# Second mixer: low parts of weights by VectorE, splits ahead of time, and a new spread of the recurrences' tasks

## The chip, the cores and the metric

One core of a Trainium2 chip. The metric is the time of the whole program on the device, in microseconds (us). TensorE multiplies matrices, VectorE and ScalarE do elementwise work on SBUF and PSUM, GpSimd elementwise work on SBUF; SyncE issues the transfers (DMA). Each engine runs its own instructions in the order in which they stand and waits at an instruction until the semaphores that it names are reached.

## The reference, cut to what matters

Two layers of a decoder trunk on 512 tokens of width 1024, float32. Each is a mixer and a mixture of experts (32 experts, top 2 of one group of 8), each with a normalisation ahead and a residual. The change stands in the second layer's mixer:

```python
def mixer_rglru(h, w_in, conv_w, conv_b, w_a, b_a, w_x, b_x, lam, w_out):
    gate, xr = jnp.split(h @ w_in, [D_RNN], axis=-1)       # (512, 1024) each
    gate = jax.nn.gelu(gate)
    xr = causal_conv(xr, conv_w) + conv_b                  # width 4, over positions
    xh = xr.reshape(bsz, t_len, LRU_HEADS, LRU_HEAD_DIM)   # 8 heads of 128
    r = jax.nn.sigmoid(einsum('bthi,hij->bthj', xh, w_a) + b_a)
    i = jax.nn.sigmoid(einsum('bthi,hij->bthj', xh, w_x) + b_x)
    log_a = (LRU_C * r) * jax.nn.log_sigmoid(lam)
    a = jnp.exp(log_a)
    b = jnp.sqrt(-jnp.expm1(2.0 * log_a)) * (i * xr)
    hseq = scan over positions of  s = a * s + b
    return (gate * hseq) @ w_out
```

## The kernel before, in words

`mixer0`, the experts of layer 0, `mixer1`, the experts of layer 1, and the final normalisation follow each other. Everything in a mixer stands with channels on the 128 partitions and the 512 tokens along the free dimension.

The product `h @ w_in` of `mixer1` is made in four parts of 512 columns, called products here: product 2 (columns of heads 0 to 3), product 3 (heads 4 to 7), then product 0 and product 1 (the gate's columns of the same heads). Each is one call of `unit`. It runs over eight row blocks of 128 rows (`j`), and a row block is 12 matmuls of 128x512: four column tiles (`m`) by three terms. The weight `w` is split for that: a high part `wh`, a cast by ScalarE (line 391), and a low part `wl = w - wh`, a subtraction by another engine (line 392); `h` is split the same way into `hh` and `hl`. The terms are high by high, high by low, low by high. In product 2 the low parts are VectorE's; in products 3, 0 and 1 they are GpSimd's (`lo=G`). `unit` splits one row block ahead: the split of block `j + 1` is written before the matmuls of block `j`. High and low parts have two buffers each, in turn. A product's four results stand in four PSUM banks, 0 to 3 for products 2 and 0, 4 to 7 for 3 and 1.

After each row block `unit` takes tasks from a list (`pump`); `queue` fills this list with one slot per row block. So the tasks of slot `j` stand, on each engine, behind the split of block `j + 1` and the matmuls of block `j`, and ahead of the split of block `j + 2`. The tasks of a head `h` are:

- `conv` (c): an ACTIVATE (line 580), then three steps on VectorE that read the product's bank (line 583).
- `gates` (g): two matmuls (line 591), a tanh by ScalarE on each (line 595). The gates of heads 4 and 5 write banks 4 and 5, where the results of product 3 for heads 4 and 5 stand until their `conv` has read them.
- `decay` (d): a tanh and an exponential by ScalarE (lines 601, 602), three steps on VectorE (lines 604 to 606).
- `newton` (w): three steps on VectorE (lines 610 to 612), the last one `q = -2q - 1`.
- `roots`: for four heads at once a table load, four square roots by ScalarE (line 616), and a load of the next table.
- `scan` (s): two steps on VectorE (lines 620, 621).
- `gated` (e): gelu of the gate by ScalarE, a product on VectorE, and the split of the result `y` into a high part (cast, line 464) and a low part (line 465) for the next product. For heads 0 to 3 GpSimd makes that low part.

Heads 0 to 3 have their conv, gates, decay and newton in product 3; heads 4 to 7 have theirs in product 0, with the scans of heads 0 to 3, and end in product 1.

Then `project` multiplies `y` by `w_out` in 16 pieces of 12 matmuls (line 691): the first two pieces need heads 0 to 3 of `y`, the next two heads 4 to 7. After them the experts' first steps are mixed in. The experts' weights come through a ring of ten buffers of 1 MB and some buffers of the mixer: the first lands in buffer `D1`, which holds heads 4 to 7 of the recurrence until the mixer's end.

Of the kernel before, what the change touches and what calls it, by code (L numbers as in the profile page):

```python
# [8 lines left out]
F32 = mybir.dt.float32  # L9
F32R = mybir.dt.float32r  # L10
# [29 lines left out]
def hybrid_trunk(ctx: ExitStack, tc: tile.TileContext, x, norm_mix_g, norm_ffn_g, norm_final_g,  # L40
# [289 lines left out]
    class Normed:  # L330
# [52 lines left out]

    par = [0]

    def split(w, lo):
        par[0] += 1
        shape = [P, *w.shape[1:]]
        wh = big.tile(shape, F32R, tag=f"w{par[0] % 2}", name="wh")
        wl = big.tile(shape, F32R, tag=f"w{par[0] % 2 + 2}", name="wl")  # L390
        A.copy(wh, w)  # L391
        lo.tensor_tensor(wl, w, f(wh), op=OP.subtract)  # L392
        return wh, wl

    first = {}

    def ahead(kind, u, lo=V):

        w = take(kind, u)
        first[kind, u] = w, split(w[:, 0, :], lo)  # L400

    def unit(kind, u, b0, step, budget=1.9, begin=lambda: None, lo=V, then=lambda: None):

        o = [bank(b0 + m, f"pu{m}") for m in range(4)]
        if (kind, u) not in first:
            ahead(kind, u, lo)
        w, nxt = first.pop((kind, u))
        begin()
        for j in range(NJ):
            wh, wl = nxt  # L410
            if j + 1 < NJ:
                if j % 4 == 3:
                    w = take(kind, u)
                nxt = split(w[:, (j + 1) % 4, :], lo)
            else:
                then()
            if j % 4 == 3:
                done()
# [27 lines left out]
    class Y:  # L446
# [13 lines left out]
        def lo(self, j):  # L460
            return self.part("D0", 4, j) if j < 4 else self.part("JK"[j // 2 - 2], 2, j % 2)
# [98 lines left out]
    def mixer1(rstd):  # L560
        n = Normed(rstd, cols[:, 88:96], 4)
        y = Y()
        step = columns_of(n)
        tags = ("t20", "t21", "sm1", "sm2")
        wax = []

        def recurrence(h0, o):

            hs = range(h0, h0 + 4)
            if h0:  # L570
                d1 = big.tile([P, 4, T], F32, tag="D1", name="xc")
# [25 lines left out]
            def decay(h):  # L597


                tt[h] = big.tile([P, T], F32, tag=tags[h - h0], name="tt")  # L600
                A.activation(tt[h], tr[h], AF.Tanh, scale=lc[:, 0, h:h + 1], bias=lc[:, 0, h:h + 1])
                A.activation(tr[h], tr[h], AF.Exp, scale=lc[:, 1, h:h + 1], bias=lc[:, 1, h:h + 1])
                q = tr[h]
                V.tensor_scalar(q, q, 0.5, 0.5, op0=OP.mult, op1=OP.add)
                V.scalar_tensor_tensor(ti[h], ti[h], 1.0, xc[h], op0=OP.add, op1=OP.mult)
                V.scalar_tensor_tensor(xc[h], tt[h], 1.0, q, op0=OP.add, op1=OP.mult)

            def newton(h):
                q = tr[h]
                V.scalar_tensor_tensor(q, xc[h], 2.0, q, op0=OP.subtract, op1=OP.mult)  # L610
                V.tensor_tensor(ti[h], ti[h], q, op=OP.mult)
                V.tensor_scalar(q, q, -2.0, -1.0, op0=OP.mult, op1=OP.add)

            def roots():
                for h in hs:
                    A.activation(tt[h], tt[h], AF.Sqrt)
                warm(AF.Gelu_apprx_tanh if h0 else AF.Exp)

            def scan(h):
                V.scalar_tensor_tensor(ti[h], ti[h], -1.0, tt[h], op0=OP.mult, op1=OP.mult)  # L620
                V.tensor_tensor_scan(xc[h], tr[h], ti[h], 0.0, op0=OP.mult, op1=OP.add)

            return conv, gates, decay, newton, roots, scan, xc

        def gated(h, o, hs, lo=V):
            if h in hs:
                A.activation(o[h % 4], o[h % 4], AF.Gelu_apprx_tanh)
                V.tensor_tensor(hs[h], o[h % 4], hs[h], op=OP.mult)
            if h - 1 in hs:
                y.put(h - 1, hs[h - 1], lo)  # L630

        def queue(*slots):

            for slot in slots:
                for i, t in enumerate(slot):
                    later(lambda t=t: t[0](*t[1:]), 1 if i + 1 == len(slot) else 0)

        o = unit("wi1", 2, 0, columns_of(n, 2), 2.0, n.begin, then=lambda: ahead("wi1", 3, G))
        c, g, d, w, roots, s, hs0 = recurrence(0, o)
        queue([(warm, AF.Exp), (c, 0)], [(c, 1)], [(g, 0), (c, 2)], [(c, 3), (g, 1)], [(d, 0), (w, 0)], [(g, 2), (d, 1), (w, 1)], [(g, 3), (d, 2), (w, 2)], [(d, 3), (w, 3)])  # L640
        o = unit("wi1", 3, 4, step, 1, lo=G, then=lambda: ahead("wi1", 0, G))
        roots0, s0 = roots, s
        c, g, d, w, roots, s, hs1 = recurrence(4, o)
        queue([(c, 4)], [(c, 5)], [(c, 6)], [(roots0,),(c, 7), (s0, 0)], [(g, 4), (s0, 1)], [(g, 5), (s0, 2), (s0, 3)], [(g, 6), (d, 4)], [(g, 7), (d, 5)])
# [12 lines left out]
        return y
# [677 lines left out]
```

## Time and profile before

| what | value |
|---|---|
| median of 3 runs | 1398.13 us (1397.18 to 1398.22) |
| the profiled execution | 1400.72 us, span 1399.0 us |
| busy in the span: TensorE | 1329.5 us (95%) |
| VectorE | 592.9 us (42%) |
| ScalarE | 350.4 us (25%) |
| GpSimd | 88.9 us (6%) |
| mean rate of transfers | 312 GB/s |

The span is the time from the first to the last record of the profiled execution; what lies around it is start and end of the program. Busy shares are means over the whole program; what the change can move is read from the stretch of `mixer1`, about 702 to 836 us of the span.

### The profile page before, as it was taken

The numbers are of one execution on the slowest core, as the hardware profiler recorded it, in microseconds if no ns is written. First come the engines' busy times: TensorE is split into PE (matmuls) and PEld (weight loads), VectorE is DVE, ScalarE is ACT, GpSimd is POOL, SyncE is SP. The second block draws the span as 40 slices with busy tenths as digits, with TensorE's granted clock in tenths as the row PEclk, the third lists the DMA queues.
The fourth block names the chain that finished last, engine by engine and source line by source line (L and its number), as shares of the span: only waits on it lengthen the run. The fifth ranks groups of instructions, "written<-read, shape, count | busy, mean of one in ns | idle before, by whom it ended". The sixth has DMA issues, their size and how long they took to land. (4 is left out here: it accounts for less than half of the span.)

```text
span 1399.0 us, 16628 instructions
## 1 busy us (share of the span) xinstructions
PE 1329.5 (95%) x6674; PEld 765.5 (55%) x6674; DVE 592.9 (42%) x1112; ACT 350.4 (25%) x592; POOL 88.9 (6%) x68
## 2 busy tenths in 40 slices
PE   9999999999999999998899889899999999999985
PEld 7888874554445544442587568645544455444432
DVE  5455462334423332322458784723333233323226
ACT  4335431221111111110247653212111111111113
POOL 0000100000000000000114332300000000000002
PEclk9999999999999999999799989999999999999997
DMA  9631169899999999999850025698999999999993
GB/s 356 184 110 60 61 227 339 348 409 409 409 408 409 409 409 409 409 409 409 299 180 0 0 75 209 219 342 345 409 409 409 409 408 409 409 409 409 409 409 142
DMA packets 126691, 436.95 MB, mean 312 GB/s; under 512 B 11284, under 2 KB 13968, under 8 KB 126608
## 3 DMA queue, kind: packets, MB, share of 16 engines
q1 hardware_dynamic: 126608, 435.82, 80.1%
q8 instruction: 55, 0.90, 0.3%
q14 instruction: 28, 0.23, 0.0%
HBM read 433.69 MB, written 2.10 MB: 311 GB/s over the span
## 5 line engine op out<-in xcount | busy, mean ns | idle before, releaser
L1008 PE MATMUL pu<-w,xt 128*64 128x512 f32 x1024 | 234.3, 597 | 20.8 <-DMA w<-in_moe_w_up_dram 20.7
L1008 PE MATMUL pg<-w,xt 128*64 128x512 f32 x1024 | 228.8, 597 | 1.2 <-DMA w<-in_moe_w_gate_dram 1.2
L1008 PE MATMUL pd<-w,hT 128*64 128x512 f32 x1024 | 226.8, 595 | 1.4 <-ACT hT L1032 1.4
L1026 DVE SCALAR_TENSOR_TENSOR hid<-pu,gs,sg 128x512 f32<-128x512 f32 x32 | 24.0, 751 | 365.6 <-PE pu L1008 245.1
L1008 PEld LDWEIGHTS pu<-w,xt 128*64 128x64 f32 x1024 | 70.0, 137 | 178.9 <-issue 120.6
L1008 PEld LDWEIGHTS pg<-w,xt 128*64 128x64 f32 x1024 | 72.8, 137 | 144.9 <-issue 134.5
L1008 PEld LDWEIGHTS pd<-w,hT 128*64 128x64 f32 x1024 | 70.7, 137 | 140.3 <-issue 129.4
L870 ACT ACTIVATE xt<-px,gcol 128x256 f32<-128x256 f32 x128 | 60.9, 476 | 303.4 <-PE px L868 303.3
L867 PE MATMUL px<-st,xh 128*128 128x256 f32 x512 | 132.8, 294 | 2.4 <-DVE st L857 2.0
L868 PE MATMUL px<-st,xl 128*128 128x256 f32 x512 | 126.6, 283 | 0.0
L867 PEld LDWEIGHTS px<-st,xh 128*128 128x128 f32 x512 | 97.9, 191 | 30.4 <-issue 26.2
L1048 ACT ACTIVATE y<-pd,gs 128x512 fp32r<-128x512 f32 x64 | 43.8, 687 | 264.6 <-PE pd L1008 263.2
L1049 DVE SCALAR_TENSOR_TENSOR y<-pd,gs,y 128x512 fp32r<-128x512 f32 x64 | 47.9, 750 | 140.9 <-ACT y L1048 138.4
L993 DVE TENSOR_TENSOR xT<-pc,xT 128x512 f32<-128x512 f32 x128 | 81.4, 684 | 57.0 <-PE pc L992 57.0
L993 DVE TENSOR_TENSOR rows<-pc,rows 128x512 f32<-128x512 f32 x128 | 81.4, 684 | 53.0 <-PE pc L992 53.0
L868 PEld LDWEIGHTS px<-st,xl 128*128 128x128 f32 x512 | 97.9, 191 | 1.6
L391 ACT CAST wh<-w 128x512 fp32r<-128x512 f32 x104 | 64.1, 619 | 68.3 <-PE pu L435 41.3
L392 DVE TENSOR_TENSOR wl<-w,wh 128x512 fp32r<-128x512 f32 x79 | 55.2, 701 | 50.8 <-PE pu L435 26.8
L435 PE MATMUL pu<-hh,wh 128*128 128x512 f32 x256 | 73.6, 409 | 2.5 <-ACT wh L391 2.0
L691 PE MATMUL po<-y,wh 128*128 128x512 f32 (+1 forms) x288 | 70.0, 385 | 5.0 <-ACT y L464 4.1
L992 PE MATMUL pc<-sp,y 128*128 128x512 f32 x256 | 69.6, 405 | 4.9 <-issue 4.9
L992 PE MATMUL pc<-y,sp 128*128 128x512 f32 x256 | 69.1, 403 | 2.2 <-DVEq L1137 2.2
(255 smaller groups left out, 1369.3 us busy)
## 6 DMA issues: line engine op xcount, KB each, us to landing
w<-in_moe_w_gate_dram SPq DMA_DIRECT2D x128, 1024.0 KB, 18.4
w<-in_moe_w_up_dram SPq DMA_DIRECT2D x128, 1024.0 KB, 18.3
w<-in_moe_w_down_dram SPq DMA_DIRECT2D x128, 1024.0 KB, 18.4
w<-in_ab_w_in_dram SPq DMA_DIRECT2D x10, 1024.0 KB, 15.1
w<-in_c_w_in_dram SPq DMA_DIRECT2D x8, 1024.0 KB, 10.9
w<-in_ab_w_out_dram SPq DMA_DIRECT2D x4, 1024.0 KB, 10.3
w<-in_c_w_out_dram SPq DMA_DIRECT2D x4, 1024.0 KB
xin<-in_x_dram SPq DMA_DIRECT2D x4, 512.0 KB, 6.7
```

What stands on the lines that cost most here:

```text
L391: A.copy(wh, w)
L392: lo.tensor_tensor(wl, w, f(wh), op=OP.subtract)
L435: TE.matmul(o[m], a[:, m * P:(m + 1) * P], b[:, j, :], start=first and i == 0, stop=last and i == 2)
L691: TE.matmul(o[m, i], w[:, kk, :], part(js[4 * kh + kk])[:, h], start=kh + k + kk == 0, stop=(kh, k, kk) == (1, 2, 3))
L867: TE.matmul(px, self.xh[:, c, j, :], st(c), start=(c == 0), stop=False)
L868: TE.matmul(px, self.xl[:, c, j, :], st(c), start=False, stop=(c == NT - 1))
L870: A.activation(self.xt[q][:, j, :], px, AF.Copy, scale=g)
L992: TE.matmul(pc, a, b, start=(n == 0), stop=(n == 1))
L993: V.tensor_tensor(d, pc, d, op=OP.add)
L1008: TE.matmul(o[64 * s:64 * s + 64, :], xt[:, 64 * s:64 * s + 64], w[s][:, j, wide], start=first, stop=last)
L1048: A.activation(yh[s], pd[s], AF.Copy, scale=by(0))
L1049: V.scalar_tensor_tensor(yl[s], pd[s], by(0), f(yh[s]), op0=OP.mult, op1=OP.subtract)
```

## The change

- `split` can write into given buffers. `unit` keeps splits in a table `rows_ahead`, so any row block may be split at any time before its matmuls; `lo` is a function of the block.
- At the end of product 2 (`while_idle`) blocks 0, 1, 2 of product 3 and blocks 0, 1 of product 0 are split, all low parts by VectorE. Blocks 2 and 3 of product 0 follow in the first two slots of product 3, by GpSimd; blocks 0 to 3 of product 1 in the last four slots of product 0, by VectorE. The buffers for these are those of `y` (`C0`, `D0`) and `D1`.
- Of the other blocks' low parts GpSimd makes blocks 3 and 4 of product 3 and block 4 of product 0, VectorE the rest. The low parts of `y` are VectorE's.
- The last step of `newton` is an ACTIVATE (Identity, scale -2, bias a column of -1).
- `queue`'s slots are new: the first roots come at the head of product 0's tasks, ahead of the convolutions; scans of heads 0 to 3 stand between the convolutions of heads 4 to 7; the gates of heads 4 to 7 come one slot earlier; the second roots, the last decays and newtons lie in product 1's first slots.
- The load of the exponential's table is put ahead of product 2.

```diff
+    minus = cons.tile([P, 1], F32, name="minus")
+    V.memset(minus, -1.0)
...
-    def split(w, lo):
-        par[0] += 1
+    def split(w, lo, into=None):
+        if into:
+            wh, wl = into
+        else:
+            par[0] += 1
...
-    def unit(kind, u, b0, step, budget=1.9, begin=lambda: None, lo=V, then=lambda: None):
+    first, halves, rows_ahead = {}, {}, {}
+
+    def row_of(kind, u, j):
+
+        if (kind, u, j // 4) not in halves:
+            halves[kind, u, j // 4] = take(kind, u)
+        return halves[kind, u, j // 4][:, j % 4, :]
+
+    def ahead(kind, u, lo=V, j=0, into=None):
+
+        rows_ahead[kind, u, j] = split(row_of(kind, u, j), lo, into)
+
+    def unit(kind, u, b0, step, budget=1.9, begin=lambda: None, lo=lambda j: V, then=lambda: None):
...
-            wh, wl = nxt
-            if j + 1 < NJ:
-                if j % 4 == 3:
-                    w = take(kind, u)
-                nxt = split(w[:, (j + 1) % 4, :], lo)
-            else:
+            wh, wl = rows_ahead.pop((kind, u, j))
+            if j + 1 == NJ:
                 then()
+            elif (kind, u, j + 1) not in rows_ahead:
+                ahead(kind, u, lo(j + 1), j + 1)
...
-                V.tensor_scalar(q, q, -2.0, -1.0, op0=OP.mult, op1=OP.add)
+                A.activation(q, q, AF.Identity, scale=-2.0, bias=minus)
...
+        def put_ahead(u, j, lo=V):
+            if j == 0:
+                shelves[u] = shelf()
+            ahead("wi1", u, lo, j, shelves[u][j])
+
+        def while_idle():
+
+            both = big.tile([P, 4, T], F32R, tag="D1", name="ahead")
+            ahead("wi1", 3)
+            for j in (1, 2):
+                ahead("wi1", 3, V, j, (both[:, j - 1], both[:, j + 1]))
+            row_of("wi1", 3, 4)
+            put_ahead(0, 0)
+            put_ahead(0, 1)
...
-        o = unit("wi1", 3, 4, step, 1, lo=G, then=lambda: ahead("wi1", 0, G))
+        o = unit("wi1", 3, 4, step, 1, lo=lambda j: G if j in (3, 4) else V)
...
-        queue([(c, 4)], [(c, 5)], [(c, 6)], [(roots0,),(c, 7), (s0, 0)], [(g, 4), (s0, 1)], [(g, 5), (s0, 2), (s0, 3)], [(g, 6), (d, 4)], [(g, 7), (d, 5)])
-        o = unit("wi1", 0, 0, step, 1, lo=G, then=lambda: ahead("wi1", 1, G))
+        queue([(roots0,), (c, 4)], [(s0, 0), (c, 5)], [(s0, 1), (c, 6)], [(g, 4), (s0, 2), (c, 7)],
+              [(g, 5), (s0, 3), (p, 1, 0)], [(g, 6), (d, 4), (p, 1, 1)], [(g, 7), (d, 5), (p, 1, 2)],
+              [(w, 4), (d, 6), (p, 1, 3)])
+        o = unit("wi1", 0, 0, step, 1, lo=lambda j: G if j == 4 else V)
...
-        queue([(d, 6)], [(d, 7), (w, 4)], [(roots,), (w, 5)], [e(0,G), (s, 4)], [e(1,G),(w, 6), (s, 5)], [e(2,G),(w, 7), (s, 6)], [e(3,G),(s, 7)], [e(4,G)])
-        o = unit("wi1", 1, 4, step, 1, lo=G, then=lambda: first_out("wo1"))
+        queue([(d, 7), (w, 5)], [(roots,), (w, 6)], [(w, 7), (s, 4)], [e(0), (s, 5)], [e(1), (s, 6)], [e(2), (s, 7)],
+              [e(3)], [e(4)])
+        o = unit("wi1", 1, 4, step, 1, then=lambda: first_out("wo1"))
```

Three places in the engines' orders follow. In them `th<-pgate` is a gate's tanh, `tt<-th` and the `th<-th,lc` behind it a head's decay on ScalarE, `wh<-w` a row block's cast, `th<-th,minus` the new last step of `newton`.

ScalarE in product 3, from the tanh of head 1's gates to the decay of head 2; before:

```order
L595 ACTIVATE th<-pgate,half 128x512 x2
L391 CAST wh<-w 128x512
L601 ACTIVATE tt<-th,lc 128x512
L602 ACTIVATE th<-th,lc 128x512
L391 CAST wh<-w 128x512
L595 ACTIVATE th<-pgate,half 128x512 x2
L601 ACTIVATE tt<-th,lc 128x512
L602 ACTIVATE th<-th,lc 128x512
L391 CAST wh<-w 128x512
```

and in the changed kernel:

```order
L602 ACTIVATE th<-pgate,half 128x512 x2
L396 CAST wh<-w 128x512
L608 ACTIVATE tt<-th,lc 128x512
L609 ACTIVATE th<-th,lc 128x512
L619 ACTIVATE th<-th,minus 128x512
L396 CAST wh<-w 128x512
L602 ACTIVATE th<-pgate,half 128x512 x2
L608 ACTIVATE tt<-th,lc 128x512
L609 ACTIVATE th<-th,lc 128x512
L619 ACTIVATE th<-th,minus 128x512
L396 CAST wh<-w 128x512
```

The last step of `newton` has come between a head's decay and the next row block's cast.

VectorE at the start of product 0, from the convolution of head 4 (`xc<-pu`) on, with buffer numbers; `th<-th,tt` and the row behind it are a scan. Before:

```order
L583 SCALAR_TENSOR_TENSOR xc_5318<-pu0_5104,cols_101,xc_5318 128x511
L583 SCALAR_TENSOR_TENSOR xc_5318<-pu0_5104,cols_101,xc_5318 128x510
L583 SCALAR_TENSOR_TENSOR xc_5318<-pu0_5104,cols_101,xc_5318 128x509
L583 SCALAR_TENSOR_TENSOR xc_5318<-pu1_5105,cols_101,xc_5318 128x511
L583 SCALAR_TENSOR_TENSOR xc_5318<-pu1_5105,cols_101,xc_5318 128x510
L583 SCALAR_TENSOR_TENSOR xc_5318<-pu1_5105,cols_101,xc_5318 128x509
```

and in the changed kernel:

```order
L590 SCALAR_TENSOR_TENSOR xc_5323<-pu0_5118,cols_103,xc_5323 128x511
L590 SCALAR_TENSOR_TENSOR xc_5323<-pu0_5118,cols_103,xc_5323 128x510
L590 SCALAR_TENSOR_TENSOR xc_5323<-pu0_5118,cols_103,xc_5323 128x509
L627 SCALAR_TENSOR_TENSOR th_5180<-th_5180,tt_5230 128x512
L628 SCALAR_TENSOR_TENSOR xc_5116<-th_5176,th_5180 128x512
L590 SCALAR_TENSOR_TENSOR xc_5323<-pu1_5119,cols_103,xc_5323 128x511
L590 SCALAR_TENSOR_TENSOR xc_5323<-pu1_5119,cols_103,xc_5323 128x510
L590 SCALAR_TENSOR_TENSOR xc_5323<-pu1_5119,cols_103,xc_5323 128x509
```

A scan of heads 0 to 3 now stands behind each convolution of heads 4 to 7. On ScalarE the first roots, which stood behind three of these heads' first ACTIVATEs, now stand ahead of all four.

ScalarE around the second roots, up to the first cast behind them; before:

```order
L601 ACTIVATE tt<-th,lc 128x512
L602 ACTIVATE th<-th,lc 128x512
L391 CAST wh<-w 128x512
L616 ACT_TABLE_LOAD
L616 ACTIVATE tt<-tt 128x512 x4
L208 ACT_TABLE_LOAD
L208 ACTIVATE dummy<-one 128x1
L391 CAST wh<-w 128x512
```

and in the changed kernel:

```order
L608 ACTIVATE tt<-th,lc 128x512
L609 ACTIVATE th<-th,lc 128x512
L396 CAST ahead<-w 128x512
L608 ACTIVATE tt<-th,lc 128x512
L609 ACTIVATE th<-th,lc 128x512
L619 ACTIVATE th<-th,minus 128x512
L623 ACT_TABLE_LOAD
L623 ACTIVATE tt<-tt 128x512 x4
L210 ACT_TABLE_LOAD
L210 ACTIVATE dummy<-one 128x1
L619 ACTIVATE th<-th,minus 128x512 x2
L396 CAST wh<-w 128x512
```

The cast at the end is that of product 1's fifth row block; three last steps of `newton` stand ahead of it, one of them ahead of the roots.

## Rows read from the trace of the kernel before

**Rows 1.** Windows: length; busy (xcount) PE, PEld, DVE, ACT, POOL; clock; DMA share, GB/s.

```profile
702.34:724.25 21.91, 21.91 (x97) 18.02 (x97) 14.78 (x23) 8.62 (x15) 1.29 (x1) 1.00 0.63 220
724.25:753.34 29.09, 29.02 (x113) 20.88 (x111) 18.03 (x26) 18.61 (x29) 9.69 (x7) 1.00 0.03 13
753.34:788.85 35.51, 31.00 (x113) 21.42 (x113) 29.74 (x34) 19.24 (x30) 13.43 (x9) 0.95 0.00 0
788.85:814.00 25.15, 23.10 (x98) 17.72 (x96) 22.79 (x25) 17.57 (x28) 14.88 (x10) 1.00 0.00 1
814.00:835.66 21.66, 15.46 (x53) 11.16 (x51) 18.51 (x25) 13.05 (x21) 3.94 (x2) 0.76 0.15 48
```

**Rows 2.** Waits of TensorE, 685 to 845 us: total, times, longest.

```profile
PE po L691 <- ACT y L464: 3.7, 1, 3.7
PE pgate L591 <- ACT th L595: 3.2, 1, 3.2
```

**Rows 3.** Timeline of ScalarE: start, us, engine, line, operation.

```profile
761.61 1.28 ACT L616 ACT_TABLE_LOAD   x1
...
766.51 0.76 ACT L580 ACTIVATE xc<-pu,cols 128x512 f32<-128x512 f32 x1
...
784.96 0.69 ACT L595 ACTIVATE th<-pgate,half 128x512 f32<-128x512 f32 x1 [0.17 <-PE pgate L591]
785.54 0.81 ACT L601 ACTIVATE tt<-th,lc 128x512 f32<-128x512 f32 x1
...
793.67 0.60 ACT L391 CAST wh<-w 128x512 fp32r<-128x512 f32 x1
```

**Rows 4.** Timeline of TensorE.

```profile
783.04 1.88 PE L591 MATMUL pgate<-xc,w 128*128 128x512 f32 x4
...
787.53 1.88 PE L591 MATMUL pgate<-xc,w 128*128 128x512 f32 x4
...
832.88 2.02 PE L691 MATMUL po<-y,wh 128*128 128x512 f32 x8
...
835.66 0.97 PE L758 MATMUL misc<-wr,xT 128*128 128x36 f32 x8
```

**Rows 5.** Timeline of VectorE.

```profile
741.62 0.43 DVE L604 TENSOR_SCALAR th<-th 128x512 f32<-128x512 f32 x1 [1.36 <-ACT th L602]
...
765.09 8.98 DVE L583 SCALAR_TENSOR_TENSOR xc<-pu,cols,xc 128x511 f32<-128x511 f32 x12
773.98 0.68 DVE L620 SCALAR_TENSOR_TENSOR th<-th,tt 128x512 f32<-128x512 f32 x1
...
775.84 0.67 DVE L620 SCALAR_TENSOR_TENSOR th<-th,tt 128x512 f32<-128x512 f32 x1
...
787.23 0.43 DVE L604 TENSOR_SCALAR th<-th 128x512 f32<-128x512 f32 x1 [4.83 <-ACT th L602]
...
798.19 0.41 DVE L604 TENSOR_SCALAR th<-th 128x512 f32<-128x512 f32 x1
...
799.31 0.69 DVE L606 SCALAR_TENSOR_TENSOR xc<-tt,th 128x512 f32<-128x512 f32 x1
799.92 0.69 DVE L610 SCALAR_TENSOR_TENSOR th<-xc,th 128x512 f32<-128x512 f32 x1
...
801.37 0.43 DVE L612 TENSOR_SCALAR th<-th 128x512 f32<-128x512 f32 x1
```

**Rows 6.** Groups by line and form, 690 to 885 us: busy us, mean ns.

```profile
L392 POOL TENSOR_TENSOR wl<-w,wh 128x512 fp32r<-128x512 f32 x24 | 36.4, 1519 | 82.1 <-ACT wh L391 80.4 <-PE pu L435 1.6
...
L392 DVE TENSOR_TENSOR wl<-w,wh 128x512 fp32r<-128x512 f32 x24 | 17.5, 729 | 5.6 <-ACT wh L391 5.6
...
L606 DVE SCALAR_TENSOR_TENSOR xc<-tt,th 128x512 f32<-128x512 f32 x8 | 11.0, 1375 | 0.8
```

**Rows 7.** Waits of the transfers' queue, 690 to 1399 us.

```profile
SPq L120 <- DVE y L465: 110.1, 1, 110.1
```

**Rows 8.** Windows as in rows 1, in the second expert layer.

```profile
1000.00:1100.00 100.00, 100.00 (x523) 50.85 (x520) 35.24 (x63) 16.14 (x29) 0.00 (x0) 1.00 1.03 409
```

More of the change, by code (lines that the diff above doesn't have):

```diff
@@ L384, in hybrid_trunk @@
     par = [0]
-    def split(w, lo):
-        par[0] += 1
-        shape = [P, *w.shape[1:]]
-        wh = big.tile(shape, F32R, tag=f"w{par[0] % 2}", name="wh")
-        wl = big.tile(shape, F32R, tag=f"w{par[0] % 2 + 2}", name="wl")
+    def split(w, lo, into=None):
[3 more added lines that the diff above has]
+            par[0] += 1
+            shape = [P, *w.shape[1:]]
+            wh = big.tile(shape, F32R, tag=f"w{par[0] % 2}", name="wh")
+            wl = big.tile(shape, F32R, tag=f"w{par[0] % 2 + 2}", name="wl")
         A.copy(wh, w)
@@ L393, in split @@
         return wh, wl
-    first = {}
-    def ahead(kind, u, lo=V):
-        w = take(kind, u)
-        first[kind, u] = w, split(w[:, 0, :], lo)
-    def unit(kind, u, b0, step, budget=1.9, begin=lambda: None, lo=V, then=lambda: None):
+    first, halves, rows_ahead = {}, {}, {}
[6 more added lines that the diff above has]
+    def unit(kind, u, b0, step, budget=1.9, begin=lambda: None, lo=lambda j: V, then=lambda: None):
         o = [bank(b0 + m, f"pu{m}") for m in range(4)]
-        if (kind, u) not in first:
-            ahead(kind, u, lo)
-        w, nxt = first.pop((kind, u))
+        if (kind, u, 0) not in rows_ahead:
+            ahead(kind, u, lo(0))
         begin()
         for j in range(NJ):
-            wh, wl = nxt
-            if j + 1 < NJ:
-                if j % 4 == 3:
-                    w = take(kind, u)
-                nxt = split(w[:, (j + 1) % 4, :], lo)
-            else:
+            wh, wl = rows_ahead.pop((kind, u, j))
+            if j + 1 == NJ:
                 then()
+            elif (kind, u, j + 1) not in rows_ahead:
+                ahead(kind, u, lo(j + 1), j + 1)
             if j % 4 == 3:
@@ L636, in queue, with begin, shelf @@
                     later(lambda t=t: t[0](*t[1:]), 1 if i + 1 == len(slot) else 0)
-        o = unit("wi1", 2, 0, columns_of(n, 2), 2.0, n.begin, then=lambda: ahead("wi1", 3, G))
+        def begin():
+            warm(AF.Exp)
+            n.begin()
+        def shelf():
+            hi, lo = (big.tile([P, 4, T], F32R, tag=t, name="ahead") for t in ("C0", "D0"))
+            return [(hi[:, k], lo[:, k]) for k in range(4)]
+        shelves = {}
+        def put_ahead(u, j, lo=V):
+            if j == 0:
+                shelves[u] = shelf()
+            ahead("wi1", u, lo, j, shelves[u][j])
@@ L639, in mixer1 @@
+        def while_idle():
[6 more added lines that the diff above has]
+            put_ahead(0, 1)
+        o = unit("wi1", 2, 0, columns_of(n, 2), 2.0, begin, then=while_idle)
         c, g, d, w, roots, s, hs0 = recurrence(0, o)
-        queue([(warm, AF.Exp), (c, 0)], [(c, 1)], [(g, 0), (c, 2)], [(c, 3), (g, 1)], [(d, 0), (w, 0)], [(g, 2), (d, 1), (w, 1)], [(g, 3), (d, 2), (w, 2)], [(d, 3), (w, 3)])
@@ L641, in mixer1 @@
-        o = unit("wi1", 3, 4, step, 1, lo=G, then=lambda: ahead("wi1", 0, G))
+        p = put_ahead
+        queue([(c, 0), (p, 0, 2, G)], [(c, 1), (p, 0, 3, G)], [(g, 0), (c, 2)], [(c, 3), (g, 1)], [(d, 0), (w, 0)],
+              [(g, 2), (d, 1), (w, 1)], [(g, 3), (d, 2), (w, 2)], [(d, 3), (w, 3)])
+        o = unit("wi1", 3, 4, step, 1, lo=lambda j: G if j in (3, 4) else V)
         roots0, s0 = roots, s
         c, g, d, w, roots, s, hs1 = recurrence(4, o)
-        queue([(c, 4)], [(c, 5)], [(c, 6)], [(roots0,),(c, 7), (s0, 0)], [(g, 4), (s0, 1)], [(g, 5), (s0, 2), (s0, 3)], [(g, 6), (d, 4)], [(g, 7), (d, 5)])
@@ L645, in mixer1 @@
-        o = unit("wi1", 0, 0, step, 1, lo=G, then=lambda: ahead("wi1", 1, G))
-        e = lambda m, lo=V: (gated, m, o, hs0, lo)
-        queue([(d, 6)], [(d, 7), (w, 4)], [(roots,), (w, 5)], [e(0,G), (s, 4)], [e(1,G),(w, 6), (s, 5)], [e(2,G),(w, 7), (s, 6)], [e(3,G),(s, 7)], [e(4,G)])
-        o = unit("wi1", 1, 4, step, 1, lo=G, then=lambda: first_out("wo1"))
+        queue([(roots0,), (c, 4)], [(s0, 0), (c, 5)], [(s0, 1), (c, 6)], [(g, 4), (s0, 2), (c, 7)],
+              [(g, 5), (s0, 3), (p, 1, 0)], [(g, 6), (d, 4), (p, 1, 1)], [(g, 7), (d, 5), (p, 1, 2)],
+              [(w, 4), (d, 6), (p, 1, 3)])
@@ L650, in freed @@
+        o = unit("wi1", 0, 0, step, 1, lo=lambda j: G if j == 4 else V)
+        e = lambda m: (gated, m, o, hs0)
+        queue([(d, 7), (w, 5)], [(roots,), (w, 6)], [(w, 7), (s, 4)], [e(0), (s, 5)], [e(1), (s, 6)], [e(2), (s, 7)],
+              [e(3)], [e(4)])
+        o = unit("wi1", 1, 4, step, 1, then=lambda: first_out("wo1"))
         def freed():
```

## Prediction

> **What bounds the kernel now.** I read the span by stages first, then who waits for whom on TensorE, and last each engine's timeline through the second mixer. The second expert layer is held by transfers: from 1000 to 1100 us the DMA moves 409 GB/s without a break [rows 8]. Its weights start on a buffer that the mixer hands back: the DMA queue's longest single wait, 110.1 us, ends with the mixer's last VectorE write of `y` [rows 7]. So what the mixer ends earlier or later, the layer behind it does too, one for one. The change stands in that mixer alone; in the rest of the program the engines' orders are the same.
>
> The mixer's first five stretches are in [rows 1]: product 2, 3, 0, 1, and the first four pieces of the output projection. Product 2 is clean: 21.91 us for eight row blocks, so 2.74 us a block. A block with the gate pair of a head takes 4.49 us (from one pair's start to the next [rows 4]), so a pair costs 1.75. Products 3 and 0 with four pairs each would need 28.9 us; the reader sees 29.09 and 35.51. Product 1 needs 21.9 and takes 25.15. A projection piece takes 2.78 us [rows 4], four of them 11.1; the stretch takes 21.66. That leaves 6.7 us over in products 3 and 0, 3.3 in product 1 and 10.5 in the projection, some 20 us, of which TensorE's idle time (length less busy) is 4.5, 2.05 and 6.2 in the last three stretches. The rest is mostly a granted clock below 1.00, part of the stretch at 1.2 in place of 2.4 GHz: 0.95 in product 0 and 0.76 in the projection, behind the two longest waits, 3.2 us for a gate's tanh and 3.7 us for `y` [rows 2].
>
> Why those waits? In product 0 VectorE is busy 29.74 of 35.51 us. It shares the work with GpSimd, whose 24 low parts take 1519 ns each where VectorE's take 729 [rows 6]. An operation of VectorE with two inputs in SBUF is longer beside one of GpSimd's: line 606 takes 1375 ns in the mean [rows 6], and 0.69 us where it stands alone, at 799.31 [rows 5]. That is 8 x 0.69 = 5.5 us of VectorE's time on that line alone.
> The Trainium skill ("SBUF — State Buffer", section "SBUF: two separate sides") says that GpSimd and a VectorE operation with two SBUF inputs shut each other out for a whole instruction; the row agrees, and by this rule alone the change should gain. That is the second rival below.
>
> **The change part by part.** *Low parts.* Of the 24 by GpSimd, 5 stay; 19 go to VectorE, and so do 4 low parts of `y`: 23 x 0.6 = 14 us more of VectorE starts (I take 0.61 from start to start, 0.69 alone). Against that go the 5.5 us of holds on line 606, those on the other two-input lines, and eight scalings of line 612. So VectorE's sum rises by less than 8.5 us, perhaps by nothing, spread over 90. The sum is not what decides.
>
> *The scaling moved to ScalarE.* The third step of `newton` becomes an ACTIVATE with a constant scale and a column as bias. The nearest row is the tanh of a gate, of the same operands: 0.69 us, the next one 0.58 behind it [rows 3]. I take 0.6 (bounds 0.5, a cast's step, and 0.75).
> The Trainium skill ("ScalarE: Activation LUTs", section "What ACT_TABLE_LOAD costs") gives about 280 + 0.833 x 512 = 707 ns for such an ACTIVATE, an estimate from that page; the sum would rise by some 0.1 us a head.
> Its length is not the price, its place is. It reads what VectorE's two earlier steps write, and it stands in ScalarE's queue ahead of the next row block's cast, the next head's tanh pair and the next head's decay. ScalarE and VectorE, which ran side by side, now take turns. Before, the cast stood directly behind the decay and waited for nobody.
>
> The walk goes by these steps [rows 3, 5]: from a head's tanh of `tt` on ScalarE to VectorE's first operation 785.54 to 787.23, 1.69; `decay` 798.19 to 799.92, 1.73; the two steps of `newton` 799.92 to 801.37, 1.45; cast 0.60; roots (two table loads, four square roots) 761.61 to 766.51, 4.90; a convolution 8.98 / 4 = 2.25; a scan pair 773.98 to 775.84, 1.86.
>
> *Product 3.* Head 0 reaches VectorE at 741.62 as before. +1.73 +1.45 = 744.80; scaling 745.4; cast of row block 6 746.0. TensorE is there at 724.25 + 6 x 2.74 + 3 x 1.75 = 745.9: 0.1 lost. Then ScalarE: two tanh (747.05), to VectorE (748.75), 3.18 (751.9), scaling (752.5), cast of row block 7 (753.1). TensorE, done with block 6 and its pair at 750.5, waits 2.6. Product 0 starts at 755.9 in place of 753.34.
>
> *Product 0.* Heads 2 and 3 go through the same turn: 753.0 + 1.16 + 1.69 + 3.18 + 0.6 = 759.65; head 3 + 1.69 + 3.18 + 0.6 = 765.1. The roots come first in the new queue: 770.0; the first convolution's own ACTIVATE 0.8, the convolution 2.25: 773.05. Before, VectorE began it at 765.09. TensorE has four blocks split ahead (755.9 + 11.0 = 766.85) and then the first gate pair, one slot earlier than before: it waits 6.2. The pair's second matmul writes the bank that the second convolution reads, and a scan pair now stands between: 1.86 + 0.7 (a GpSimd hold, line 606's mean excess) + 2.25 = 777.85, a wait of 3.95. Then block 4 (781.45) and a pair (783.2); the low part of block 5, now VectorE's, stands behind two more scan pairs and convolutions: 777.85 + 2 x 4.11 + 0.69 = 786.75, needed at 785.0: 1.7. On from there, blocks and pairs end product 0 at 796.65 in place of 788.85. The waits of products 3 and 0 are 0.1 + 2.6 + 6.2 + 3.95 + 1.7 = 14.55; before, 6.7 us were over there: 7.8 later.
>
> *Product 1.* The splits ahead cover blocks 0 to 3, until 796.65 + 10.95 = 807.6. Block 4's cast stands behind the roots, and these behind head 5's scaling. From the last pair (start 792.15): second tanh 1.92 + 0.58 (the step from 783.04 to 784.96 [rows 3, 4]) = 794.65; + 1.69; VectorE decay, one low part, newton 1.73 + 0.6 + 1.45 = 800.1; scaling 800.7; + 1.69 = 802.4; decay, low part, decay, newton 5.5 = 807.9; scaling 808.5; roots 813.4; two scalings 814.6; cast 815.2. TensorE waits 7.6. Blocks 4 to 7 take 10.95; VectorE owes 0.6 + 0.6 + 0.6 + 1.86 = 3.7 a block there against TensorE's 2.74, less its lead: 0 to 2.8 lost, I take 1.0. End at 827.2; before, 814.0.
>
> *Projection.* Its first two pieces (5.6 us) cover ScalarE's two table loads (2 x 1.28), gelu and casts; then `y` of heads 4 to 7 comes about 0.3 us a part slower than TensorE takes it. Bounds 0 and the 6.2 idle of before; I take 2.5. 827.2 + 11.1 + 2.5 = 840.8; before, 835.66 [rows 4]: 5.2 later. So of 13.2 us that come late, 8 come back, since the old waits and the slow clock at the projection go.
>
> *Clock.* In product 0 a granted clock of 0.95 cost 0.05 x 35.5 = 1.8 us behind 4.5 us of idle time. Behind 10 us of it I expect 1.8 to 3.5, of which the 1.7 wait for block 5's low part hides half; behind the 7.6 wait the later waits hide it. I add 0.8.
>
> *What costs nothing.* The table load put ahead of product 2 and the five splits at its end lie where ScalarE and VectorE wait for TensorE (8.62 and 14.78 us busy of 21.91). The weights are there: no transfers run in products 3, 0 and 1. If that cover were gone, a split would cost its 0.7. The constant for the bias is one small memset ahead of the first load's landing.
>
> **Sum.** 5.2 + 0.8 = 6.0 us. The profiled execution took 1400.72 (span 1399.0 and 1.7 around it), 2.6 above the median; it would take 1406.7, the median 1398.13 + 6.0 = 1404.1.
>
> **Rivals.** *The same turn-taking, and more of it* (10 in 100): the clock after the long waits stays low into product 1, and `y` costs the full 6.2: 6.0 + 3.7 + 1.0 = 10.7, and up to 1409 to 1411. For it: 0.76 in the old projection behind 3.7 us; against it: VectorE is then behind anyway.
>
> *Faster* (7 in 100): VectorE, free of GpSimd's holds, ends each `newton` before ScalarE comes to the scaling, and the splits ahead cover products 0 and 1. Then 4.5 + 2.05 of idle time and 1.8 of clock go, the projection's waits stay: -8.4, 1389.8. It holds if the scaling and its wait take ScalarE less than the 1.2 us a head that it has to spare (4.49 less two tanh 1.16, the decay some 1.6 and a cast 0.5). For it: line 606's 5.5 us. Against it: the turn, 3.18 us of VectorE, starts only when ScalarE has ended the same head's decay, so it can't be over when the next instruction in the queue is the scaling.
>
> *No change* (10 in 100): the three long waits are as told, but a turn is shorter by 0.5 us a head and the projection gives back all of its 10.5: 1398 within 0.2% (2.8 us, about what can be told from no change here). It needs 4 to 6 us less on the chain.
>
> **The numbers.** The forecast's own case has 73 in 100. Its lower end: no wait for `y`, none on VectorE in product 1, no clock: 6.0 - 2.5 - 1.0 - 0.8 = 1.7, 1399.8. Its upper end with the first rival's price: 1408.8. The range 1399.5 to 1409 leaves out the faster rival, part of no change and the top of the first rival. Slower by over 0.2% 0.82, within 0.10, faster 0.08.
>
> **What would show it.** Each step has its sign: ScalarE idle some 3 us a head ahead of line 619 in products 3 and 0, waiting for line 618; TensorE waiting about 2.6 us for a cast near 750, 6 and 4 us at line 598's first gate pair, 7 to 8 us for `wh` in the fifth block of product 1; the projection nearly free of waits. I am wrong if ScalarE does not wait at line 619, if convolution of head 4 begins before 768, or if product 1 has no long wait; the time is then at or below 1398.

## The result, and the profile after

The changed kernel takes 1406.69 us (median of 5 runs, 1404.46 to 1409.77) where the kernel before takes 1397.86 beside it: 8.8 us slower, ratio 1.0066, 95% interval 1.0054 to 1.0077. The profiled execution took 1409.51, also 8.8 more than the 1400.72 of before. The forecast was 6.0 slower (1404.1, range 1399.5 to 1409).

Of the 8.8 us, 7.8 arise in the second mixer: from product 2's start to the first router block of the projection 141.14 us, before 133.32. Product 2 itself starts 0.8 earlier (701.51, before 702.34), and the stretch behind, up to the last down product, is 1.8 longer (536.7, before 534.9). The five stretches after, to be laid beside [rows 1]:

```profile
701.51:723.42 21.91, 21.91 (x96) 18.04 (x97) 16.60 (x26) 10.46 (x19) 0.00 (x0) 1.00 0.69 245
723.42:755.55 32.13, 29.52 (x113) 20.92 (x112) 18.36 (x29) 17.60 (x28) 5.10 (x4) 1.00 0.03 11
755.55:797.52 41.97, 32.88 (x113) 22.52 (x112) 27.79 (x39) 22.55 (x34) 1.26 (x1) 0.84 0.00 0
797.52:829.23 31.71, 24.32 (x98) 19.37 (x96) 25.94 (x40) 19.21 (x31) 0.00 (x0) 0.89 0.00 1
829.23:842.65 13.42, 12.21 (x52) 9.07 (x51) 8.81 (x15) 10.62 (x18) 0.00 (x0) 1.00 0.23 74
```

Product 3 is 3.0 us longer, product 0 6.5, product 1 6.6, the projection's start 8.2 shorter. The slow clock has moved from the projection (0.76) into products 0 and 1. VectorE's busy time over the five fell from 103.85 to 97.5 us, though it has 23 more low parts. It is rid of eight scalings (6.3 us in the kernel before, 790 ns each) and of GpSimd's company on most other lines. So it isn't the sum that grew.

TensorE's waits in the mixer after (total, times, longest), against [rows 2]:

```profile
PE pu L442 <- ACT wh L396: 9.9, 2, 7.4
PE pgate L598 <- DVE xc L590: 9.1, 2, 6.3
...
PE po L729 <- ACT y L471: 1.0, 2, 0.7
PE po L729 <- ACT wh L396: 0.2, 1, 0.2
```

ScalarE's timeline through product 3 and the start of product 0 (brackets: idle before, and what ended it) shows where they come from; compare [rows 3]:

```profile
740.10 0.81 ACT L609 ACTIVATE th<-th,lc 128x512 f32<-128x512 f32 x1
744.19 0.72 ACT L619 ACTIVATE th<-th,minus 128x512 f32<-128x512 f32 x1 [3.27 <-DVE th L618]
744.82 0.60 ACT L396 CAST wh<-w 128x512 fp32r<-128x512 f32 x1
...
751.40 0.72 ACT L619 ACTIVATE th<-th,minus 128x512 f32<-128x512 f32 x1 [3.27 <-DVE th L618]
752.03 0.60 ACT L396 CAST wh<-w 128x512 fp32r<-128x512 f32 x1
...
764.32 0.72 ACT L619 ACTIVATE th<-th,minus 128x512 f32<-128x512 f32 x1 [3.35 <-DVE th L618]
765.04 1.28 ACT L623 ACT_TABLE_LOAD   x1
...
769.94 2.10 ACT L587 ACTIVATE xc<-pu,cols 128x512 f32<-128x512 f32 x3
```

Six of the eight scalings (L619), these three among them, find ScalarE idle for about 3.3 us until VectorE's second newton step (L618) has ended. The cast at 752.03 is ready only then, and TensorE starts block 7 at 752.68. The roots begin at 765.04, the convolution's ACTIVATE behind them at 769.94. Over the whole execution (busy us, mean ns, then idle ahead) this one line owns

```profile
L619 ACT ACTIVATE th<-th,minus 128x512 f32<-128x512 f32 x8 | 5.7, 718 | 20.0 <-DVE th L618 20.0
```

TensorE's timeline at its four waits, and the slow blocks behind two of them; compare [rows 4]:

```profile
752.68 1.20 PE L442 MATMUL pu<-hh,wh 128*128 128x512 f32 x4 [2.47 <-ACT wh L396]
...
773.19 2.05 PE L598 MATMUL pgate<-xc,w 128*128 128x512 f32 x2 [6.29 <-DVE xc L590]
778.04 2.05 PE L598 MATMUL pgate<-xc,w 128*128 128x512 f32 x2 [2.80 <-DVE xc L590]
779.10 2.70 PE L442 MATMUL pu<-hh,wh 128*128 128x512 f32 x4
...
784.05 1.88 PE L598 MATMUL pgate<-xc,w 128*128 128x512 f32 x4
...
816.27 2.08 PE L442 MATMUL pu<-hh,wh 128*128 128x512 f32 x4 [7.39 <-ACT wh L396]
...
821.05 1.09 PE L442 MATMUL pu<-hh,wh 128*128 128x512 f32 x4
```

Behind the second wait a block takes 4.95 us (779.10 to 784.05), behind the last 4.78, where a block at full clock takes 2.74.

### The profile page after: what moved, and what is told of

The parts are those of the page before. It is cut to its first block, busy times and chain, and to the rows that moved or that the text cites. A ratio compares the mean times of both kernels' runs of the same rounds, so it can differ in the third digit from the quotient of the medians.

```text
span 1407.8 us, 16606 instructions
## 1 busy us (share of the span) xinstructions
PE 1326.4 (94%) x6674; PEld 763.8 (54%) x6674; DVE 586.4 (42%) x1128; ACT 354.8 (25%) x600; POOL 51.7 (4%) x45
## 5 line engine op out<-in xcount | busy, mean ns | idle before, releaser
L1046 PEld LDWEIGHTS pd<-w,hT 128*64 128x64 f32 x1024 | 70.7, 137 | 140.4 <-issue 129.3
L908 ACT ACTIVATE xt<-px,gcol 128x256 f32<-128x256 f32 x128 | 60.7, 475 | 302.1 <-PE px L906 302.1
L397 DVE TENSOR_TENSOR wl<-w,wh 128x512 fp32r<-128x512 f32 x90 | 61.7, 687 | 58.2 <-PE pu L442 26.8
L396 ACT CAST wh<-w 128x512 fp32r<-128x512 f32 x94 | 58.1, 621 | 67.5 <-PE pu L442 41.9
L442 PE MATMUL pu<-hh,wh 128*128 128x512 f32 x216 | 63.3, 416 | 10.4 <-ACT wh L396 9.9
L1062 ACT ACTIVATE sg<-pg,gs 128x512 f32<-128x512 f32 x32 | 22.0, 687 | 193.3 <-PE pg L1046 186.2
```

The lines of the kernel that those rows point to most:

```text
L908: A.activation(self.xt[q][:, j, :], px, AF.Copy, scale=g)
L1046: TE.matmul(o[64 * s:64 * s + 64, :], xt[:, 64 * s:64 * s + 64], w[s][:, j, wide], start=first, stop=last)
```

## Experiments

Theory A: the scaling's place in ScalarE's queue makes the two engines take turns. B: the first roots, put ahead of the convolutions, delay the gates. C: VectorE's added low parts are the cost. Each time is a median beside the kernel before on the same chip (1397.8 to 1398.4), with the difference from it. "Mixer" is the length from product 2's start to the first router block in the profile; before has 133.3, the changed kernel 141.1.

**1. Scaling back on VectorE, the rest as changed.**

```diff
-                A.activation(q, q, AF.Identity, scale=-2.0, bias=minus)
+                V.tensor_scalar(q, q, -2.0, -1.0, op0=OP.mult, op1=OP.add)
```

> The changed kernel with one line undone: newton's last step (times -2, minus 1) goes back to VectorE. Theory A (turns): ScalarE stands idle 3.3 us ahead of this step for each of six heads of the changed kernel, 20 us in all, and whatever is queued behind it (casts, roots, the next head's tanh) comes late. Without it the 2.5 us wait near 750 goes, the two waits at the first gate pairs (6.3 and 2.8) shrink since the first roots start some 7 us earlier, and the 7.4 us wait of product 1 shrinks to under 2 since the second roots do too. That is 2.5 + 6.3 + 2.8 + 5.5 = 17 us of waits less at most, of which the projection takes some back: 12 to 16 us faster than the changed kernel, 1391 to 1395. Rival B (the order: first roots ahead of the convolutions): the two gate waits stay, only 2.5 + part of 7.4 go: 1400 to 1403. Rival C (VectorE, which got 18 more low parts of weights and 4 of y, is the bound): the eight scalings come back to it, 0.4 us each, so no gain or a loss: 1406 to 1410.

1391.84, 6.6 faster than before (ratio 0.9958, 0.9944 to 0.9972); mixer 126.4. One line is worth 14.7 us of the mixer. Of the two gate waits one is left, with 2.6 us, and VectorE's low parts are now waited for:

```profile
PE pu L442 <- DVE wl L397: 5.3, 5, 2.6
PE pgate L598 <- DVE xc L590: 2.6, 1, 2.6
```

**2. The kernel before with the scaling on ScalarE alone** (experiment 1's edit reversed).

> The kernel before with one line of the change alone: newton's last step is done by ScalarE, with the column of minus ones as bias. Theory A (turns): in products 3 and 0 each head's cast then stands behind a 3.3 us wait. Product 3 has four such heads inside the product or behind it, and the kernel before has no blocks split ahead to cover them: it loses at least the 2.5 us of the changed kernel's product 3, and again for each later head whose cast is needed at once, 4 to 9 us in all: 1402 to 1407. Rival B (the order): 1398 to 1399, since the order stays that of before. Rival C (VectorE's sum): 1395 to 1398, since VectorE loses eight steps.

1403.74, 5.3 slower (1.0043, 1.0030 to 1.0057); mixer 139.9. In the kernel before TensorE waits once for a cast in these products; here it waits eight times. The rows before and after:

```profile
PE pu L435 <- ACT wh L391: 2.0, 1, 2.0
```

```profile
PE pu L437 <- ACT wh L393: 15.6, 8, 4.3
```

The scaling owns 25.3 us of ScalarE's idle time:

```profile
L614 ACT ACTIVATE th<-th,minus 128x512 f32<-128x512 f32 x8 | 5.8, 720 | 25.3 <-DVE th L613 25.3
```

**3. The changed kernel with product 0's tasks in the old order**, the scaling still on ScalarE.

```diff
-        queue([(roots0,), (c, 4)], [(s0, 0), (c, 5)], [(s0, 1), (c, 6)], [(g, 4), (s0, 2), (c, 7)],
...
+        queue([(c, 4)], [(c, 5)], [(c, 6)], [(roots0,),(c, 7), (s0, 0)], [(g, 4), (s0, 1), (p, 1, 0)],
...
```

> The changed kernel with the tasks of product 0 in the order of the kernel before (the three first convolutions ahead of the first roots, gates a slot later), the splits ahead for product 1 in the slots of the four gate pairs; the scaling stays on ScalarE, product 1's order stays that of the changed kernel. It tells what the place of the first roots costs by itself. Theory A with B as its second half: the convolutions start at once, so the gate waits of 6.3 and 2.8 us go; the turns of product 3 (2.5) stay: 4 to 8 us faster than the changed kernel, 1399 to 1403. Turns alone, the order costing nothing: within 2 us of the changed kernel, 1405 to 1409. Rival C: no difference from the changed kernel either.

1402.06, 3.7 slower than before (1.0039, 1.0025 to 1.0052), 4.6 faster than the changed kernel; mixer 135.7. The gate waits of 6.3 and 2.8 are gone, a wait of 2.2 us for a low part has come in, the cast waits stay, and the one of product 1 has grown from 7.4 to 9.3:

```profile
753.52 2.08 PE L442 MATMUL pu<-hh,wh 128*128 128x512 f32 x4 [2.43 <-ACT wh L396]
...
811.63 2.08 PE L442 MATMUL pu<-hh,wh 128*128 128x512 f32 x4 [9.28 <-ACT wh L396]
```

**4. Both undone**: experiments 1 and 3 together, and product 1's tasks in the old order too.

> The changed kernel with both undone: the scaling on VectorE, and the tasks of products 0 and 1 in the order of the kernel before (with the splits ahead in the slots of the four gate pairs of product 0). What is left of the change is the splits ahead into the output's buffers and the low parts by VectorE. If A and B are the causes, neither is left, and the splits ahead take away what the kernel before still waits for: the idle 4.5 and 2.05 us of products 0 and 1, the 1.8 us of slow clock, and a part of the projection's 6.2: 6 to 11 us faster than the kernel before, 1387 to 1392. Rival C (VectorE's larger load is the cost): slower than the kernel before, 1399 or more.

1389.95, 8.4 faster (0.9943, 0.9929 to 0.9956); mixer 123.9. What is left of the change, splits ahead and low parts by VectorE, gains. C falls.

**5. The kernel before with the mixer's low parts by VectorE**, nothing else.

```diff
-        o = unit("wi1", 0, 0, step, 1, lo=G, then=lambda: ahead("wi1", 1, G))
+        o = unit("wi1", 0, 0, step, 1, then=lambda: ahead("wi1", 1))
...
```

> The kernel before with the low parts of the second mixer (24 of weights, 4 of y) by VectorE and nothing else changed: no splits ahead, order and scaling as before. It tells how much of the 8.4 us that the fourth experiment gained comes from freeing VectorE of GpSimd, and how much from the splits ahead. If the holds of GpSimd cost VectorE more than the low parts do (line 606 alone 5.5 us, rows of before), the waits of products 0 and 1 that come from VectorE shrink: 1391 to 1394. If the splits ahead are what gained: 1397 to 1400. Rival C (VectorE's load): 1400 to 1405.

1393.16, 4.6 faster (0.9961, 0.9948 to 0.9974); mixer 127.9. So of experiment 4's 8.4 us some 4.6 come from freeing VectorE; by difference, the splits ahead add the rest. Line 606, 1375 ns in [rows 6], now reads

```profile
L606 DVE SCALAR_TENSOR_TENSOR xc<-tt,th 128x512 f32<-128x512 f32 x8 | 5.5, 692 | 0.4
```

The Trainium skill ("SBUF — State Buffer", section "SBUF: two separate sides") says that GpSimd and a VectorE operation with two SBUF inputs exclude each other; these 692 against 1375 ns agree. An operation with one input was longer too, the scaling; before and here:

```profile
L612 DVE TENSOR_SCALAR th<-th 128x512 f32<-128x512 f32 x8 | 6.3, 790 | 0.3
```

```profile
L612 DVE TENSOR_SCALAR th<-th 128x512 f32<-128x512 f32 x8 | 3.4, 427 | 0.3
```

The convolution's steps, which read a PSUM bank, take 742 to 749 ns before and 745 to 748 here.

**6. The kernel before with the new order alone.**

```diff
-        queue([(c, 4)], [(c, 5)], [(c, 6)], [(roots0,),(c, 7), (s0, 0)], [(g, 4), (s0, 1)], ...
+        queue([(roots0,), (c, 4)], [(s0, 0), (c, 5)], [(s0, 1), (c, 6)], [(g, 4), (s0, 2), (c, 7)], ...
...
```

> The kernel before with the new order of the tasks of products 0 and 1 alone (first roots ahead of the convolutions, gates a slot earlier, newton of heads 4 to 7 earlier), without splits ahead; low parts by GpSimd and scaling by VectorE as before. If the place of the first roots costs something only where the turns have made them late (the roots of before started at 761.61, when TensorE was in product 0's fourth block): 1396 to 1400. If the place costs by itself what the third experiment gained (4.6 us): 1401 to 1404.

1397.55, no difference (0.9998, 0.9989 to 1.0007); mixer 131.7, in a profile of the fastest of 11 runs (1394.08). So B alone changes nothing in the total, but the place isn't free: TensorE now waits twice for a cast, 4.5 us in product 0 and 3.8 in product 1,

```profile
PE pu L435 <- ACT wh L391: 8.3, 2, 4.5
```

and product 1 ends 116.4 us behind product 2's start, where the kernel before has 113.4. The projection gives it back: 15.3 us to the first router block, before 19.9. With the scaling on VectorE the new order costs nothing here and 1.9 us with splits ahead (experiments 4 to 1); with it on ScalarE 3.7 (2 to 7) and 4.6 (3 to the changed kernel). It is dearest where the turns have made the roots late.

**7. The new order and the scaling on ScalarE on the kernel before**, as the edits of 6 and 2.

> The kernel before with the new order and the scaling on ScalarE, without splits ahead and with low parts by GpSimd as before: the changed kernel less its splits and its low parts. By the theory of turns and late roots, both costs stand here without the cover of four blocks split ahead: 8.8 us as the changed kernel, and on top some 2 to 6 us that splits ahead and freed VectorE gave it: 1408 to 1413. If splits and low parts are what made the changed kernel slow: 1398 to 1402.

1407.39, 9.6 slower (1.0063, 1.0050 to 1.0076); mixer 142.8. It is slower, as A with B wants, but below the forecast 1408: with the scaling on ScalarE, splits ahead and low parts by VectorE are worth only 0.7 us (1407.39 to 1406.69), less than the runs of one kernel spread; with it on VectorE, in the same order, 5.7 (1397.55 to 1391.84). What TensorE waits for here are casts, and neither splits ahead nor low parts take work out of ScalarE's queue (argued, not tested by itself):

```profile
PE pu L437 <- ACT wh L393: 16.4, 8, 3.3
```

**8. The changed kernel with TensorE's two long waits filled** by products with a block of zeros.

```diff
             step(o, wh, wl, j, j == 0, j == NJ - 1)
+            if fill and j == 3:
+                for k in range(fill[1]):
+                    TE.matmul(o[k % 4][0:64], zero, fill[0].hh[:, 0, :], start=False, stop=False)
```

> The changed kernel, with matrix products by a block of zeros added to the open banks of TensorE where its two long waits are: 24 of them ahead of the first gate pair of product 0 (wait 6.3 us, 24 x 0.227 = 5.4 us) and 28 ahead of the fifth block of product 1 (wait 7.4 us, 6.4 us). They add nothing to the result and end before the data come. If the slow clock behind these waits (blocks of 4.95 and 4.78 us in place of 2.74, and a gate pair of 2.05) costs by itself: 1402.5 to 1405, some 2 to 4 us faster than the changed kernel, less what the low part of the next block then makes late (1.7). If the waits for ScalarE and VectorE alone set the end: 1406 to 1408, the same.

1409.71 (1406.65 to 1411.06), 11.9 slower than before (1.0076, 1.0064 to 1.0088); mixer 142.5. It is no faster than the changed kernel, and above both forecasts. In product 0 the clock isn't tested: the first gate pair runs at full clock (1.10 us), but TensorE then waits longer for the second, 3.75 us where it was 2.80, and block 4 takes 4.85 us again:

```profile
777.28 2.04 PE L603 MATMUL pgate<-xc,w 128*128 128x512 f32 x2 [3.75 <-DVE xc L595]
```

In product 1 the clock does rise from 0.89 to 1.00, and the fifth block takes 2.86 us:

```profile
807.85 6.63 PE L431 MATMUL pu<-hh,zero 128*64 128x512 f32 x28
815.41 1.19 PE L447 MATMUL pu<-hh,wh 128*128 128x512 f32 x4 [0.93 <-ACT wh L398]
...
818.27 1.07 PE L447 MATMUL pu<-hh,wh 128*128 128x512 f32 x4
...
836.79 2.50 PE L734 MATMUL po<-y,wh 128*128 128x512 f32 x5 [0.72 <-ACT y L476]
```

Product 1 then ends 1.0 us earlier, counted from product 2's start (126.7 against 127.7), but the last parts of `y` come when they came before. VectorE's last row of them here, and in the changed kernel (with two low parts of weights ahead of it):

```profile
836.00 1.46 DVE L477 TENSOR_TENSOR y<-xc,y 128x512 fp32r<-128x512 f32 x2
```

```profile
819.32 0.67 DVE L397 TENSOR_TENSOR wl<-w,wh 128x512 fp32r<-128x512 f32 x1
...
822.96 0.67 DVE L397 TENSOR_TENSOR wl<-w,wh 128x512 fp32r<-128x512 f32 x1
...
836.87 1.46 DVE L472 TENSOR_TENSOR y<-xc,y 128x512 fp32r<-128x512 f32 x2
```

Their last rows are 135.25 and 135.36 us behind product 2's start. TensorE waits longer in the projection instead (1.08 us for a cast of its weights, there 0.20; then 1.0 us for `y` in both) and goes slow there: the clock of the projection's stretch is 0.89, in the changed kernel 1.00, and five matmuls at 836.79 take 2.50 us, there 1.43. So VectorE sets when `y` comes in both, and the slow block of product 1 cost nothing; but a slow clock behind the last wait for `y` does cost, since nothing covers it: the mixer is 1.3 us longer.

**9. The changed kernel with the scaling still on ScalarE, but at the head of the scan.**

```diff
             def newton(h):
...
-                A.activation(q, q, AF.Identity, scale=-2.0, bias=minus)
...
             def scan(h):
+                A.activation(tr[h], tr[h], AF.Identity, scale=-2.0, bias=minus)
```

> The changed kernel with its eight scalings still on ScalarE, the same instruction of 0.72 us, but issued later: at the head of each scan, behind the roots, not at the end of newton. Nothing else is changed. If the place in ScalarE's queue is the price (a wait of 3.3 us ahead of each, with casts, tanh and roots queued behind it), the wait is gone, since VectorE's two steps are long done by then: as fast as the first experiment (scaling on VectorE, 1391.8) or up to 3 us faster, since VectorE saves 0.34 us a head where it is waited for: 1388 to 1392. If the 0.72 us themselves, 5.8 us more work for ScalarE, are the price: 1400 to 1406.

1389.28, 9.1 faster than before (0.9936, 0.9924 to 0.9949); mixer 125.3. The same eight instructions of the same length, on the same engine, now have nothing ahead of them:

```profile
L626 ACT ACTIVATE th<-th,minus 128x512 f32<-128x512 f32 x8 | 5.7, 714 | 0.0
```

So the price was the place, not ScalarE's added 5.7 us. The kernel is 17.4 us faster than the changed one.

**10. The parts that gained, together** (the scaling as in experiment 9; the new slots of products 0 and 1 below).

```diff
+        queue([(c, 4)], [(c, 5)], [(c, 6)], [(roots0,),(c, 7), (s0, 0)], [(g, 4), (s0, 1), (p, 1, 0)],
...
+        queue([(d, 6), (w, 4)], [(d, 7), (w, 5)], [(roots,), (w, 6)], [e(0), (s, 4), (w, 7)], [e(1), (s, 5)],
...
```

> The parts that gained, together: splits ahead and low parts by VectorE as in the changed kernel, the order of the kernel before in product 0 (convolutions ahead of the first roots), newton of heads 4 to 7 one row block earlier in product 1, and the scaling on ScalarE at the head of the scan. The fourth experiment (1390.0) still waits 5.7 us for VectorE's low parts, three of them in product 1, where VectorE has a newton, a scan, a gated product and two low parts a block; the scaling off VectorE and the newtons ahead take 0.34 and up to 1.8 us a block there: 2 to 4 us faster than the fourth experiment, 1386 to 1388. If the scaling's place mattered less than supposed and ScalarE becomes the engine waited for: 1390 to 1394.

1386.42 (1384.76 to 1387.45), 11.9 faster than before (0.9915, 0.9902 to 0.9928), 3.5 faster than experiment 4; mixer 121.9, the shortest of all. It beats both kernels. TensorE's longest waits in products 3, 0 and 1 are now

```profile
PE pu L442 <- DVE wl L397: 2.9, 4, 1.1
...
PE pu L442 <- ACT wh L396: 0.7, 1, 0.7
```

## Why the prediction was right, step by step

*The scaling's place: right.* "Some 3 us a head" are 3.25 to 3.48, at six heads; experiments 1, 2 and 9 show it as cause: the same line costs 5.3 us in the kernel before (experiment 2), 14.9 in the changed one (1). From its start to that of the next instruction 0.6 was taken; it is 0.63 ahead of a cast and 0.72 ahead of the table load. Its own length is 0.72, near the estimate of 707 ns by the Trainium skill ("ScalarE: Activation LUTs", section "What ACT_TABLE_LOAD costs"). Four turns, each 0.1 to 0.2 longer than taken, and a convolution 0.2 longer bring the first gate pair 71.7 us behind product 2's start where 70.7 was forecast.

*The four long waits: right in place and cause.* 2.47, 6.29, 2.80 and 7.39 us, forecast 2.6, 6.2, 3.95 and 7.6. The third is shorter because the pair ahead of it took 2.05 us at the slow clock. The fifth, 1.7 for a low part, did not come: the slow pair and block 4 (4.95 us) made TensorE so late that the low part was done 1.0 us before it was read:

```profile
785.95 0.68 DVE L397 TENSOR_TENSOR wl<-w,wh 128x512 fp32r<-128x512 f32 x1
```

```profile
787.61 1.09 PE L442 MATMUL pu<-hh,wl 128*128 128x512 f32 x4
```

*The clock: about right.* 0.8 us were added. In product 0 the second pair and block 4 took 6.0 us (778.04 to 784.05) where 3.6 were reckoned: 2.4 more, inside the expected 1.8 to 3.5. The 1.7 us wait that was to hide half of it is the one that did not come, so 0.7 is left. With 1.0 from the longer turns, product 0 ended 1.7 us later than the walk had it (96.0 us behind product 2's start, against 94.3). Product 1 lost 2.0 us in one block (4.78 for 2.74). The forecast had 1.0 there for VectorE, which needs 3.64 us a block (from one low part to the next, 819.32 to 822.96; 3.7 was forecast). Experiment 8, without the slow block, ends product 1 1.0 us earlier and gets `y` no earlier: the clock's time and VectorE's are the same time, and hidden, as the forecast had it.

*The projection: right.* Forecast 13.6 us, measured 13.42, with 1.2 us of waits; 8.2 of the earlier loss came back, forecast 8.0.

*VectorE's sum: wrong sign, no consequence.* "Rises by less than 8.5, perhaps by nothing": it fell by 6.3. The eight scalings, 6.3 us at the 790 ns that they took beside GpSimd, are all of that. The added low parts took 14.5 us, and nearly as much came back on lines that GpSimd had held: 5.5 on line 606, 2.4 and 2.0 on lines 610 and 611, 1.9 on the scan (line 621), the rest on others.

*One for one into the expert layer: not exact.* The mixer's loss was 7.8, forecast 6.0. Stage by stage against the walk, product 3 is 0.5 longer, product 0 1.2, product 1 1.2 and the projection 0.2 shorter: 2.7, of which the 0.8 for the clock had been added. The stretch behind gave 1.8 more, and product 2's start 0.8 less; neither was forecast, so that the 8.8 us hold 1.0 that the mixer does not explain. The stretch behind is between 533.6 and 536.7 us long in twelve profiles of kernels that are alike there, and the changed kernel's is the longest. Experiments 7 and 8, whose mixers end as late, have 534.3 and 533.7, so a late mixer doesn't lengthen it by itself; what did is not shown. In the changed kernel's profile a part of it is visible at the third gate product of the experts: the rows that it reads (L908) come from ScalarE, where a table load stands ahead of them,

```profile
914.03 1.28 ACT L210 ACT_TABLE_LOAD   x1
...
915.43 0.82 ACT L908 ACTIVATE xt<-px,gcol 128x256 f32<-128x256 f32 x2
```

```profile
915.94 3.63 PE L1046 MATMUL pg<-w,xt 128*64 128x512 f32 x8 [2.51 <-ACT xt L908]
```

and the product then runs at the slow clock (3.63 us; the next one takes 1.94). The transfers' queue still waits for the mixer's `y`, now 118.0 us against the 110.1 of [rows 7]:

```profile
SPq L120 <- DVE y L472: 118.0, 1, 118.0
```

*The rivals.* "Faster" was excluded by the turn; the same gain that it named (GpSimd's holds) is real, 4.6 us in experiment 5, and is what the changed kernel loses again. "More of the same" reckoned with 1408.8, and 1406.69 lies about halfway between it and the 1404.1 of the forecast. Its cause isn't what happened: the clock was low, 0.84 and 0.89, but blocks 5 to 7 of product 1 ran at full clock (2.7 us each), and `y` cost 1.2 us, not 6.2.

What stays open: why the runs of one kernel spread by 3 to 5 us. Product 2 starts between 698.3 and 702.3 us in the twelve profiles, behind a first layer that no kernel here touches; no run was made on that.

## What to carry to other kernels

Eight instructions moved to an engine that had time to spare cost nothing here by their length and up to 17.4 us by their place: ask what stands behind such an instruction in that engine's queue, and issue it where its input is long done. Splits made ahead, with low parts by VectorE, helped little where the engine that makes them was itself held in waits (0.7 us, against 5.7 without the waits). And before adding a slow clock to a sum, look whether another engine's chain ends the stretch anyway: in product 1 it did, at the projection it did not.

## What the runs showed of the hardware

With products by a block of zeros in TensorE's wait ahead of product 1's fifth block the granted clock was 1.00 through product 1 (experiment 8); with the engine idle there it was 0.89. The slow clock came back at the next waits that were left open (0.89 in that run's projection). With GpSimd making low parts, VectorE's line 606, two inputs in SBUF, took 1375 ns in the mean and 692 without; line 612, one input, 790 and 427; the convolution, one input in PSUM, 742 to 749 and 745 to 748 (experiment 5).
